# Summing the weights of the first MLP product on VectorE and GpSimd instead of in adding transfers

## The chip, the cores and the metric

The kernel runs on one core of one Trainium2 chip. The metric is the time of one execution in microseconds (us); less is better. Beside the engines the text speaks of queues: SP's queue issues plain loads, POOL's queue issues stores, the transfers that add into what they write, and whatever GpSimd computes. Both work strictly in the order in which their instructions stand. In the rows of the profile PE is TensorE, PEld its weight loads, DVE VectorE, ACT ScalarE, POOL GpSimd, and SPq or POOLq the issuing side of a queue.

## The reference

One layer of a hybrid backbone over 512 latent positions of width 2048, with 256 context tokens before them. What matters here is its last part:

```python
def squared_relu_mlp(h, w1, w2):
    return jnp.square(jax.nn.relu(h @ w1)) @ w2
...
xl = xl + gt2_l * squared_relu_mlp(modulate(rms_norm(xl, g_mlp[l]), sh2_l, sc2_l), w_mlp1[l], w_mlp2[l])
return rms_norm(xl, g_final)
```

`h` is 512x2048, `w1` 2048x8192 and `w2` 8192x2048, all in float32. Ahead of it stand the adaLN modulation (`silu(c) @ w_ada + b_ada`, six vectors of 2048), an input projection, a Fourier group, a state-space scan and an output projection. The last of the six modulation vectors, the gate `gt2_l`, is needed only in the second product.

## The kernel before

**Exact products by three passes.** A weight tile of 128x1024 is loaded raw and split into two parts, `whi` (ScalarE casts it, L84) and `wlo` (VectorE subtracts, L85). `mm3` (L106 to L108) then multiplies hi by hi, lo by hi and hi by lo. A weight tile can be used by TensorE only once its `wlo` is there, and the pool of split tiles holds three pairs: the split of a tile starts when TensorE has finished the tile three places before it.

**Seven products for eight.** Both MLP products cut the matrices into 2x2 blocks and use seven block products with sums of weight blocks in place of eight. `seven` (L858) delivers the seven weight tiles of one row of work in the order that its loop gives them. This text calls them by number, in that order: item 1 (block 11), 2 (block 12), 5 (the sum s of blocks 21 and 22), 6 (s plus block 11), 4 (block 22), 7 (block 21 plus block 11), 3 (s plus blocks 11 and 12). An item is 24 matmuls (8 pieces of 128, three passes), so a row is 168 matmuls. Items 6 and 3 are made by VectorE additions in place (`s_2`, L873, and `s_4`, L877). The two other sums, for items 5 and 7, are made by transfers: `load` with two blocks issues a plain load on SP's queue (L869) and then, on POOL's queue, one that adds a second block from HBM into the same tile (L867). A row thus moves seven blocks of 512 KB: five plain and two adding.

**The two stages.** The first product runs 32 rows. Three of them are done in a different way beforehand, from wide slabs of weights (`w_1s`, split at L99 and L100), while the activations are still being made; 29 rows go through `seven(w_1[...])`. Each ends with a store of its 512 KB of hidden values on POOL's queue (L931). The second product runs 8 chunks of 4, again through `seven`; its transfers and additions are not touched by the change.

**Other work in the rows.** The gate vector is computed in the background: `background(2)` at the end of a row runs two steps of `ada_rest` (L194 to L206). A step loads a tile of 512 KB on SP's queue and makes two VectorE passes over it into `adacc` (L200, one of each eight L198); after eight steps TensorE reduces the result with eight small matmuls (L204). There are 32 steps, so the first 16 of the 29 rows carry them and the last 13 do not. Below these are called gate rows and plain rows, and a gate row's tiles gate tiles. The first activations of the second product (`hr`, four loads, L951) are also loaded during rows 1 and 2.

**Buffers and order.** Raw weights and gate tiles share one pool of seven tiles of 512 KB. A scheduler assigns a free tile when it places an instruction and fixes the order on each engine; `tc.high_priority()` puts the weight work first. An instruction at the head of an engine's queue that waits holds up everything behind it on that engine.

Of the kernel before, what the change touches and what calls it, by code (L numbers as in the profile page):

```python
# [10 lines left out]
ALU = mybir.AluOpType  # L11
# [25 lines left out]
N1P = 3  # L37
# [17 lines left out]
def tile_hybrid_trunk(ctx, tc, xT, ctxT, cvec, ccol, vec, alog, w_ada, w_adr, w_ins, w_zs, w_in, w_dt, w_f, w_o,  # L55
                      w_1s, w_1, w_2, cst, sel_d, dft, cw_d, out):
    nc = tc.nc
    v = nc.vector
    s = nc.scalar
# [14 lines left out]
    def acc(n=L):  # L74
        return psa.tile([P, L], F32, name="acc")[:, :n]

    def bank():
        return psb.tile([P, 512], F32, name="bank")

    def split(raw):  # L80

        hi = pools["ws"].tile([P, HALF], F32R, name="whi")
        lo = pools["ws"].tile([P, HALF], F32R, name="wlo")
        s.copy(hi, raw)  # L84
        v.tensor_sub(lo, raw, hi.bitcast(F32))  # L85
        return hi, lo

    def raw_tile():
        return pools["wp"].tile([P, HALF], F32, name="wraw")
# [15 lines left out]
    def mm3(ps, a, b, first, last, on=False):  # L105
        te.matmul(ps, a[0], b[0], start=first, stop=False, skip_group_check=on)  # L106
        te.matmul(ps, a[1], b[0], start=False, stop=False, skip_group_check=on)  # L107
        te.matmul(ps, a[0], b[1], start=False, stop=last, skip_group_check=on)  # L108
# [168 lines left out]
    def background(n):  # L277
        for _ in range(min(n, len(todo))):
            todo.pop(0)()
# [265 lines left out]
    for g in range(NG):  # L545
        b_tok = cp.tile([P, NCC, P], F32, name="cb_tok")
        x_tok = cp.tile([P, NCC, HG * 64], F32, name="cx_tok")
        for i in range(4):
            t = T_B + g if i == 0 else T_X + g * 3 + i - 1
# [216 lines left out]
    def sumsq(accum, x, pool, k):  # L766
        if k == 0:
            s.activation(accum, x, AF.Square)
        else:
            q = pool.tile([P, L], F32, name="nq")  # L770
            s.activation(q, x, AF.Square)
            v.tensor_add(accum, accum, q)
# [82 lines left out]
    for ci in range(20, 24):  # L855
        todo.extend(ada_rest(ci, None, stg1))

    def seven(src, use):  # L858

        raw = {}  # L860

        def load(n, *ij):
            raw[n] = raw_tile()
            for a, (i, j) in enumerate(ij):
                d = src[i, j].rearrange("p a b -> p (a b)" if len(src.shape) == 5 else "p a b c -> p (a b c)")
                if a:
                    nc.gpsimd.dma_start(out=raw[n], in_=d, accum_op=ALU.add)  # L867
                else:
                    nc.sync.dma_start(out=raw[n], in_=d)  # L869
            return raw[n]  # L870

        def s_2():
            v.tensor_add(raw["s"], raw["s"], raw["11"])  # L873
            return raw["s"]

        def s_4():
            v.tensor_add(raw["s"], raw["s"], raw["12"])  # L877
            return raw["s"]

        for n, f in ((1, lambda: load("11", (0, 0))), (2, lambda: load("12", (0, 1))),  # L880
                     (5, lambda: load("s", (1, 0), (1, 1))), (6, s_2), (4, lambda: load("22", (1, 1))),
                     (7, lambda: load("t", (1, 0), (0, 0))), (3, s_4)):
            with tc.high_priority():
                w = split(f())
            use(n, w)
# [9 lines left out]
    for rr in range(N1P, NP):  # L895
        ct = stg.tile([P, 4, LC], F32, name="ct")
        sn = stg.tile([P, 4, LC], F32, name="sn")
        ps = {}

        def use(n, w):  # L900
            if n == 1:
                ps["x"] = acc(LC)
            elif n in (2, 5, 4):
                ps[{2: "y", 5: "z", 4: "w"}[n]] = bank()[:, :LC]
            o = ps[{1: "x", 6: "x", 7: "x", 2: "y", 5: "z", 3: "z", 4: "w"}[n]]
            for k in range(8):
                sl = slice(k * P, (k + 1) * P)
                i, q = k // QC, k % QC
                mm3(o, (w[0][:, sl], w[1][:, sl]), (chi[i][:, SLOT[n], q], clo[i][:, SLOT[n], q]),
                    k == 0 and n not in (6, 7, 3), k == 7, n not in (2, 4))  # L910
            if n == 1:
                s.copy(sn[:, 0], o)
            elif n == 2:
                v.tensor_add(ct[:, 0], sn[:, 0], o)
            elif n == 5:
                s.copy(sn[:, 3], o)
            elif n == 6:
                s.copy(sn[:, 1], o)
            elif n == 4:
                s.copy(sn[:, 2], o)  # L920
            elif n == 7:
                v.tensor_sub(ct[:, 2], o, sn[:, 2])
                v.tensor_add(ct[:, 3], o, sn[:, 3])
            else:
                v.tensor_add(ct[:, 1], sn[:, 1], o)

        seven(w_1[rr - N1P], use)
        s.activation(ct[:, 2:4], ct[:, 2:4], AF.Relu, scale=-1.0)
        s.activation(ct[:, 0:2], ct[:, 0:2], AF.Relu)
        s.activation(ct, ct, AF.Square)  # L930
        nc.gpsimd.dma_start(out=hid_d[rr // QC][:, :, rr % QC], in_=ct)  # L931
        background(2)
# [52 lines left out]
    for c in range(NFC):  # L985
        hi, lo = chi[c % 2], clo[c % 2]
        last = c == NFC - 1
        if last:
            hr_stack.close()
            comb0_stack.close()  # L990
            fin["p"] = ctx.enter_context(tc.tile_pool(name="fin", bufs=2))
            x2p = ctx.enter_context(tc.tile_pool(name="x2p", bufs=1))
            x2f = [x2p.tile([P, L], F32, name=f"x2f{j}") for j in range(KT)]
            fin["a"] = fin["p"].tile([P, L], F32, name="na2")
            fin["r"] = fin["p"].tile([P, L], F32, name="na2")
            for j in range(KT):
                jj = j // 2 + (j % 2) * 8
                nc.sync.dma_start(out=x2f[jj], in_=x2_d[jj])
        else:
            todo.extend(factors(c + 1))  # L1000
        for op in range(4):
            cts = [[stc.tile([P, 2, LC], F32, name=f"ca{i}{o}") for i in range(2)] for o in range(2)]
            sns = [stc1.tile([P, 3, LC], F32, name=f"sn{o}") for o in range(2)]
            pss = [{}, {}]

            def use2(n, w):
                wv = [w_.rearrange("p (q o m) -> p q o m", q=QC, o=2) for w_ in w]
                for o in range(2):
                    ps, ct, sn = pss[o], cts[o], sns[o]
                    j = 2 * op + o  # L1010
                    if n == 1:
                        ps["x"] = acc(LC)
                    elif n in (2, 5, 4):
                        ps[{2: "y", 5: "z", 4: "w"}[n]] = bank()[:, :LC]
                    d = ps[{1: "x", 6: "x", 7: "x", 2: "y", 5: "z", 3: "z", 4: "w"}[n]]
                    for q in range(QC):
                        mm3(d, (wv[0][:, q, o], wv[1][:, q, o]), (hi[:, SLOT[n], q], lo[:, SLOT[n], q]),
                            q == 0 and n not in (6, 7, 3), q == QC - 1, n not in (2, 4))
                    g0, g1, n1 = mod[:, 80 + j:81 + j], mod[:, 88 + j:89 + j], ng[:, j:j + 1]
                    if n == 1:  # L1020
                        s.activation(sn[:, 0], d, AF.Copy, scale=g0)
                    elif n == 2:
                        v.scalar_tensor_tensor(ct[0][:, 0], d, g0, sn[:, 0], ALU.mult, ALU.add)  # L1023
                    elif n == 5:
                        s.activation(sn[:, 2], d, AF.Copy, scale=g1)
                    elif n == 6:
                        s.activation(sn[:, 0], d, AF.Copy, scale=g0)
                    elif n == 4:
                        s.activation(sn[:, 1], d, AF.Copy, scale=g1)
                    elif n == 7:  # L1030
                        v.scalar_tensor_tensor(ct[1][:, 0], d, n1, sn[:, 1], ALU.mult, ALU.add)
                        v.scalar_tensor_tensor(ct[1][:, 1], d, n1, sn[:, 2], ALU.mult, ALU.subtract)
                    else:
                        v.scalar_tensor_tensor(ct[0][:, 1], d, g0, sn[:, 0], ALU.mult, ALU.add)

            seven(w_2[c, op], use2)
            for o in range(2):
                for i in range(2):
                    j = 2 * op + o + 8 * i
                    ct = cts[o][i].rearrange("p a b -> p (a b)")  # L1040
                    if last:
                        v.tensor_add(x2f[j], x2f[j], ct)
                        sumsq(fin["a"], x2f[j], fin["p"], op + o + i)
                    else:
                        nc.gpsimd.dma_start(out=x2_d[j], in_=ct, accum_op=ALU.add)
            background(2)
        background(len(todo))
# [86 lines left out]
```

## Time and profile before

| | us |
|---|---|
| median of 3 runs | 2385.83 (2382.52 to 2394.14) |
| the profiled execution | 2374.16 |
| its span (first to last instruction) | 2372.4 |
| TensorE busy in the span | 2262.6 (95%) |
| VectorE busy | 1811.1 (76%) |
| ScalarE busy | 1176.3 (50%) |
| GpSimd busy | 285.7 (12%) |
| adding weight loads in both MLP products | 122, of these 58 in the first |

The rows of the first product begin with TensorE at about 1072 us and end at about 1703 us; the second product follows to the end. One instruction marks the rows well: ScalarE's copy at L912, which stands once in every row, right after the row's first item. In a row of the trace's order of time the columns are start, duration, engine, line, operation, tiles and shapes, count, and in brackets the idle time ahead of it with what ended it. In a row of a grouped view they are busy time and mean nanoseconds, then the idle time before the group's instructions with what ended it.

### The profile page before, as it was taken

The numbers are of one execution on the slowest core, as the hardware profiler recorded it, in microseconds if no ns is written. First come the engines' busy times: TensorE is split into PE (matmuls) and PEld (weight loads), VectorE is DVE, ScalarE is ACT, GpSimd is POOL, SyncE is SP. The second block draws the span as 40 slices with busy tenths as digits, with TensorE's granted clock in tenths as the row PEclk, the third lists the DMA queues.
The fourth block names the chain that finished last, engine by engine and source line by source line (L and its number), as shares of the span: only waits on it lengthen the run. The fifth ranks groups of instructions, "written<-read, shape, count | busy, mean of one in ns | idle before, by whom it ended". The sixth has DMA issues, their size and how long they took to land.

```text
span 2372.4 us, 38829 instructions
## 1 busy us (share of the span) xinstructions
PE 2262.6 (95%) x15242; PEld 2004.8 (85%) x15242; DVE 1811.1 (76%) x2551; ACT 1176.3 (50%) x1646; POOL 285.7 (12%) x375
## 2 busy tenths in 40 slices
PE   6999999999999999898999999999999999999996
PEld 2347789877777777698999989999999999999995
DVE  7978779987778677675666666666898887888778
ACT  4125245456555422254444545555665665566554
POOL 0000000000000000111101101111122222222210
PEclk9999999999999999999999999999999999999998
DMA  8988877823224499557888877777899999999993
GB/s 297 333 296 299 330 240 261 279 83 122 83 63 148 144 345 303 187 163 230 253 224 244 239 217 220 208 209 213 242 264 267 266 250 267 259 265 247 242 267 116
DMA packets 163456, 544.72 MB, mean 230 GB/s; under 512 B 19284, under 2 KB 20196, under 8 KB 163016
## 3 DMA queue, kind: packets, MB, share of 16 engines
q1 hardware_dynamic: 115624, 402.35, 49.6%
q0 software_dynamic: 46496, 137.79, 27.1%
q8 instruction: 119, 1.95, 0.3%
q10 hardware_dynamic: 1152, 2.10, 0.2%
q14 instruction: 65, 0.53, 0.1%
HBM read 479.24 MB, written 62.92 MB: 229 GB/s over the span
## 4 chain that ended last, share of the span: by engine, by line
PE 63%; DVE 15%; DMA 14%; issue 4%; ACT 3%; SPq 0%; DVEq 0%; POOL 0%; ACTq 0%; POOLq 0%
PE acc L107 10%; PE acc L108 10%; PE acc L106 9%; PE bank L107 8%; PE bank L106 8%; PE bank L108 8%; DMA araw<-in_w_ada_dram 5%; DMA wraw<-in_w_adr_dram 3%; DVE araw L172 3%; DVE wlo L100 2%; DVE wlo L85 2%; DMA araw<-in_w_adr_dram 2%; DMA wraw<-in_w_o_dram 1%; PE bank L347 1%; PE bank L667 1%
## 5 line engine op out<-in xcount | busy, mean ns | idle before, releaser
L85 DVE TENSOR_TENSOR wlo<-wraw,whi 128x1024 fp32r<-128x1024 f32 x427 | 519.4, 1221 | 224.0 <-ACT whi L84 221.1
L84 ACT CAST whi<-wraw 128x1024 fp32r<-128x1024 f32 x427 | 445.4, 1048 | 448.8 <-PE bank L108 158.4
L107 PE MATMUL bank<-chi,wlo 128*128 128x256 f32 (+1 forms) x2000 | 569.7, 285 | 6.1 <-DVE wlo L85 6.1
L106 PE MATMUL bank<-chi,whi 128*128 128x256 f32 (+1 forms) x2000 | 569.6, 285 | 1.1 <-DVE ca L1023 0.8
L108 PE MATMUL bank<-clo,whi 128*128 128x256 f32 (+1 forms) x2000 | 569.3, 285 | 0.0
L107 PE MATMUL acc<-chi,wlo 128*128 128x256 f32 (+1 forms) x1512 | 435.7, 288 | 21.7 <-DVE wlo L85 21.5
L106 PE MATMUL acc<-chi,whi 128*128 128x256 f32 (+1 forms) x1512 | 433.4, 287 | 7.3 <-ACT chi L830 6.7
L108 PE MATMUL acc<-clo,whi 128*128 128x256 f32 (+1 forms) x1512 | 433.7, 287 | 0.0
L107 PEld LDWEIGHTS bank<-chi,wlo 128*128 128x128 f32 x2000 | 384.5, 192 | 7.7 <-DVE wlo L85 6.7
L106 PEld LDWEIGHTS bank<-chi,whi 128*128 128x128 f32 x2000 | 384.5, 192 | 2.6 <-DVE ca L1023 1.3
L108 PEld LDWEIGHTS bank<-clo,whi 128*128 128x128 f32 x2000 | 384.5, 192 | 0.9
L107 PEld LDWEIGHTS acc<-chi,wlo 128*128 128x128 f32 x1512 | 293.6, 194 | 25.7 <-DVE wlo L85 24.3
L106 PEld LDWEIGHTS acc<-chi,whi 128*128 128x128 f32 x1512 | 293.1, 194 | 9.5 <-ACT chi L830 7.6
L107 PE MATMUL acc<-bh,wlo 128*128 128x512 f32 x720 | 286.2, 397 | 13.3 <-DVE wlo L100 13.3
L108 PEld LDWEIGHTS acc<-clo,whi 128*128 128x128 f32 x1512 | 293.5, 194 | 1.6 <-DVE clo L832 0.6
L106 PE MATMUL acc<-bh,whi 128*128 128x512 f32 x720 | 285.3, 397 | 1.1 <-ACT whi L99 1.1
L108 PE MATMUL acc<-bl,whi 128*128 128x512 f32 x720 | 284.4, 395 | 0.0
L99 ACT CAST whi<-wraw 128x1024 fp32r<-128x1024 f32 (+2 forms) x145 | 142.7, 987 | 263.3 <-PE acc L108 228.6
L867 POOL DMA_DIRECT2D wraw<-in_w_dram x122 | 105.1, 861 | 757.1 <-DMA wraw<-in_w_dram 334.8
L100 DVE TENSOR_TENSOR wlo<-wraw,whi 128x1024 fp32r<-128x1024 f32 (+2 forms) x145 | 165.6, 1144 | 29.0 <-ACT whi L99 28.0
L107 PEld LDWEIGHTS acc<-bh,wlo 128*128 128x128 f32 x720 | 136.1, 189 | 48.2 <-DVE wlo L100 20.1
L106 PEld LDWEIGHTS acc<-bh,whi 128*128 128x128 f32 x720 | 136.0, 189 | 29.8 <-ACT whi L99 1.6
(336 smaller groups left out, 3274.0 us busy)
## 6 DMA issues: line engine op xcount, KB each, us to landing
wraw<-in_w_dram SPq DMA_DIRECT2D x305, 512.0 KB, 5.2
araw<-in_w_ada_dram SPq DMA_DIRECT2D x164, 512.0 KB, 6.7
wraw<-in_w_dram POOLq DMA_DIRECT2D x122, 512.0 KB, 8.0
wraw<-in_w_in_dram SPq DMA_DIRECT2D x84, 512.0 KB, 4.5
x<-ca POOLq DMA_DIRECT2D x112, 256.0 KB, 8.0
araw<-in_w_adr_dram SPq DMA_DIRECT2D x48, 512.0 KB, 4.6
wraw<-in_w_adr_dram SPq DMA_DIRECT2D x32, 512.0 KB, 7.7
hid<-ct POOLq DMA_DIRECT2D x32, 512.0 KB, 5.4
```

The source lines that it names most:

```text
L84: s.copy(hi, raw)
L85: v.tensor_sub(lo, raw, hi.bitcast(F32))
L99: s.copy(hi, raw)
L100: v.tensor_sub(lo, raw, hi.bitcast(F32))
L106: te.matmul(ps, a[0], b[0], start=first, stop=False, skip_group_check=on)
L107: te.matmul(ps, a[1], b[0], start=False, stop=False, skip_group_check=on)
L108: te.matmul(ps, a[0], b[1], start=False, stop=last, skip_group_check=on)
L172: v.tensor_tensor_reduce(o, a, cond[:, hf * HALF:(hf + 1) * HALF], 1.0, last if hf else first, ALU.mult, ALU.add, dst[:, ch:ch + 1] if hf ...
L347: te.matmul(a[:n], w[:, o:o + n], tmp, start=k == 0, stop=k == KT - 1)
L667: te.matmul(py[hh * 64:hh * 64 + 64, c * P:(c + 1) * P], xd[d][:, c, hh], ms[2 * hh + d][:, c], start=c == 0 and d == 0, stop=c == NCH - 1 ...
L867: nc.gpsimd.dma_start(out=raw[n], in_=d, accum_op=ALU.add)
```

## The change

In the first product, `seven` no longer loads sums. Blocks 21 and 22 are loaded plain, once each (tiles `t` and `22`); VectorE adds them into a new tile `s` for item 5 (`s_1`), item 4 uses the tile `22` that is already there, and for item 7 GpSimd adds block 11 into `t` in place (`s_3`). The second product keeps its adding transfers (`adds=True`).

```diff
-    def seven(src, use):
+    def seven(src, use, adds):
...
+        def s_1():
+            if adds:
+                return load("s", (1, 0), (1, 1))
+            load("t", (1, 0))
+            load("22", (1, 1))
+            raw["s"] = raw_tile()
+            v.tensor_add(raw["s"], raw["t"], raw["22"])
+            return raw["s"]
+
+        def w_22():
+            return load("22", (1, 1)) if adds else raw["22"]
+
+        def s_3():
+            if adds:
+                return load("t", (1, 0), (0, 0))
+            nc.gpsimd.tensor_tensor(raw["t"], raw["t"], raw["11"], ALU.add)
+            return raw["t"]
...
-        for n, f in ((1, lambda: load("11", (0, 0))), (2, lambda: load("12", (0, 1))),
-                     (5, lambda: load("s", (1, 0), (1, 1))), (6, s_2), (4, lambda: load("22", (1, 1))),
-                     (7, lambda: load("t", (1, 0), (0, 0))), (3, s_4)):
+        for n, f in ((1, lambda: load("11", (0, 0))), (2, lambda: load("12", (0, 1))), (5, s_1), (6, s_2), (4, w_22),
+                     (7, s_3), (3, s_4)):
             with tc.high_priority():
                 w = split(f())
             use(n, w)
...
-        seven(w_1[rr - N1P], use)
+        seven(w_1[rr - N1P], use, False)
...
-            seven(w_2[c, op], use2)
+            seven(w_2[c, op], use2, True)
```

A row now moves four blocks, all on SP's queue. Line numbers shift: L873 and L877 become L891 and L895, L914 becomes L931, L922 to L925 become L939 to L942, and L931 becomes L948. The order of TensorE's and ScalarE's work is unchanged. The order of three other engines follows, for the turn from one gate row to the next, the same row of the program before and after.

VectorE before, from the addition for item 3 (L877) to the split of the next row's item 2:

```order
L877 TENSOR_TENSOR wraw_9857<-wraw_9857,wraw_9825 128x1024
L85 TENSOR_TENSOR wlo_9923<-wraw_9920,whi_9922 128x1024
L85 TENSOR_TENSOR wlo_9956<-wraw_9952,whi_9955 128x1024
L85 TENSOR_TENSOR wlo_9987<-wraw_9857,whi_9986 128x1024
L200 SCALAR_TENSOR_TENSOR adacc_9782<-wraw_10255,cs_79,adacc_9782 128x512 x2
L85 TENSOR_TENSOR wlo_10032<-wraw_10029,whi_10031 128x1024
L200 SCALAR_TENSOR_TENSOR adacc_9782<-wraw_10259,cs_79,adacc_9782 128x512
L922 TENSOR_TENSOR ct_9791<-acc_9799,sn_9792 128x256
L923 TENSOR_TENSOR ct_9791<-acc_9799,sn_9792 128x256
L85 TENSOR_TENSOR wlo_10064<-wraw_10061,whi_10063 128x1024
```

VectorE in the changed program, the same stretch:

```order
L895 TENSOR_TENSOR wraw_9856<-wraw_9856,wraw_9820 128x1024
L85 TENSOR_TENSOR wlo_9919<-wraw_9854,whi_9918 128x1024
L85 TENSOR_TENSOR wlo_9950<-wraw_9852,whi_9949 128x1024
L878 TENSOR_TENSOR wraw_10091<-wraw_10087,wraw_10089 128x1024
L85 TENSOR_TENSOR wlo_9981<-wraw_9856,whi_9980 128x1024
L200 SCALAR_TENSOR_TENSOR adacc_9777<-wraw_10248,cs_79,adacc_9777 128x512 x2
L85 TENSOR_TENSOR wlo_10026<-wraw_10023,whi_10025 128x1024
L200 SCALAR_TENSOR_TENSOR adacc_9777<-wraw_10252,cs_79,adacc_9777 128x512
L939 TENSOR_TENSOR ct_9786<-acc_9794,sn_9787 128x256
L940 TENSOR_TENSOR ct_9786<-acc_9794,sn_9787 128x256
L85 TENSOR_TENSOR wlo_10058<-wraw_10055,whi_10057 128x1024
```

The splits of items 4, 7 and 3 stand as before; the new addition (L878) for the next row's item 5 stands between those of items 7 and 3, and waits there for the next row's blocks 21 (`wraw_10087`) and 22 (`wraw_10089`).

SP's queue before, the loads of one row and its two gate tiles:

```order
L869 DMA wraw_10029<-in_w_1_dram 128x1024
L869 DMA wraw_10061<-in_w_1_dram 128x1024
L869 DMA wraw_10093<-in_w_1_dram 128x1024
L869 DMA wraw_10156<-in_w_1_dram 128x1024
L869 DMA wraw_10188<-in_w_1_dram 128x1024
L194 DMA wraw_10255<-in_w_adr_dram 128x1024
L194 DMA wraw_10259<-in_w_adr_dram 128x1024
```

SP's queue in the changed program:

```order
L869 DMA wraw_10023<-in_w_1_dram 128x1024
L869 DMA wraw_10055<-in_w_1_dram 128x1024
L869 DMA wraw_10087<-in_w_1_dram 128x1024
L869 DMA wraw_10089<-in_w_1_dram 128x1024
L194 DMA wraw_10248<-in_w_adr_dram 128x1024
L194 DMA wraw_10252<-in_w_adr_dram 128x1024
```

The load for item 7 is gone from between the block 22 and the gate tiles. In both programs the first gate tile takes the buffer that the split of the preceding row's item 7 gives free, and the second the one that item 3's split gives free. In the changed program block 21 takes a buffer that the preceding row's addition for item 6 (L891) and GpSimd's addition leave, and block 22 one that the addition for item 3 (L895) leaves.

POOL's queue before, and then in the changed program, for the same rows:

```order
L867 DMA wraw_10093<-in_w_1_dram 128x1024
L867 DMA wraw_10188<-in_w_1_dram 128x1024
L931 DMA hid2_6732<-ct_9791 512x1x256
L867 DMA wraw_10329<-in_w_1_dram 128x1024
L867 DMA wraw_10424<-in_w_1_dram 128x1024
```

```order
L887 TENSOR_TENSOR wraw_10087<-wraw_10087,wraw_10023 128x1024
L948 DMA hid2_6732<-ct_9786 512x1x256
L887 TENSOR_TENSOR wraw_10322<-wraw_10322,wraw_10258 128x1024
L948 DMA hid2_6732<-ct_10021 512x1x256
L887 TENSOR_TENSOR wraw_10563<-wraw_10563,wraw_10499 128x1024
```

Two adding loads per row have become one addition, in front of the same store. It waits for L878 of its own row, which reads the tile that it overwrites.

## The prediction

> **What bounds the kernel now.** I first read the summary of engines. TensorE is busy for 95% of the span, so the change can only win where TensorE waits or runs slowly.
>
> ```profile
> PE 2262.6 (95%) x15242; PEld 2004.8 (85%) x15242; DVE 1811.1 (76%) x2551; ACT 1176.3 (50%) x1646; POOL 285.7 (12%) x375
> ```
>
> Next comes the order of time on ScalarE, where L912 marks each row of the first product: the first gate rows, then the first plain rows.
>
> ```profile
> 1075.00 0.37 ACT L912 COPY sn<-acc 128x256 f32<-128x256 f32 x1
> 1102.36 0.36 ACT L912 COPY sn<-acc 128x256 f32<-128x256 f32 x1
> 1129.25 0.37 ACT L912 COPY sn<-acc 128x256 f32<-128x256 f32 x1
> ...
> 1439.04 0.37 ACT L912 COPY sn<-acc 128x256 f32<-128x256 f32 x1 [1.05 <-PE acc L108]
> 1459.20 0.37 ACT L912 COPY sn<-acc 128x256 f32<-128x256 f32 x1 [0.16 <-PE acc L108]
> 1479.36 0.37 ACT L912 COPY sn<-acc 128x256 f32<-128x256 f32 x1 [0.16 <-PE acc L108]
> ```
>
> A plain row takes 20.16 us, which is 168 matmuls at 0.12 us: TensorE never waits there, and no saved transfer can make it shorter. The 16 gate rows take 1439.04 - 1075.00 = 364.04 us, where 16 x 20.16 = 322.56 would do. The excess is 41.5 us, 7.2 of it in row 0 (27.36 us) and 6.7 in row 1 (26.89 us). What it consists of, by TensorE's groups in these rows and by stretches around the wait in row 1 (columns: busy us of PE, PEld, DVE, ACT, POOL with counts, then granted clock, DMA share, GB/s):
>
> ```profile
> L107 PE MATMUL bank<-chi,wlo 128*128 128x256 f32 x512 | 146.0, 285 | 6.1 <-DVE wlo L85 6.1
> L107 PE MATMUL acc<-chi,wlo 128*128 128x256 f32 x376 | 110.4, 294 | 21.0 <-DVE wlo L85 21.0
> L204 PE MATMUL bank<-ones,adacc 128*128 128x2 f32 x32 | 3.8, 241 | 0.0
> ...
> 1118.00:1124.00 6.00, 0.00 (x0) 0.00 (x0) 2.62 (x4) 0.00 (x0) 0.85 (x1) 0.84 1.05 391
> 1124.00:1127.00 3.00, 2.94 (x13) 2.94 (x14) 3.00 (x6) 1.57 (x2) 0.00 (x0) 0.50 1.02 287
> 1130.00:1134.00 4.00, 4.00 (x36) 4.00 (x35) 3.03 (x4) 1.99 (x2) 0.28 (x1) 1.00 0.70 204
> ```
>
> TensorE waits 27.1 us for VectorE's `wlo`; the gate's own small matmuls are at most 3.8. Most of the rest is clock: after the wait in row 1 the granted clock is 0.50, and 13 matmuls pass in 3 us instead of 25. Why `wlo` is late shows on VectorE, in the turn between two gate rows:
>
> ```profile
> 1311.13 1.22 DVE L877 TENSOR_TENSOR wraw<-wraw 128x1024 f32<-128x1024 f32 x1
> 1312.27 1.22 DVE L85 TENSOR_TENSOR wlo<-wraw,whi 128x1024 fp32r<-128x1024 f32 x1
> 1313.96 1.23 DVE L85 TENSOR_TENSOR wlo<-wraw,whi 128x1024 fp32r<-128x1024 f32 x1 [0.48 <-ACT whi L84]
> 1316.89 1.22 DVE L85 TENSOR_TENSOR wlo<-wraw,whi 128x1024 fp32r<-128x1024 f32 x1 [1.70 <-ACT whi L84]
> 1322.92 1.54 DVE L200 SCALAR_TENSOR_TENSOR adacc<-wraw,cs,adacc 128x512 f32<-128x512 f32 x2 [4.81 <-DMA wraw<-in_w_adr_dram]
> 1324.37 1.22 DVE L85 TENSOR_TENSOR wlo<-wraw,whi 128x1024 fp32r<-128x1024 f32 x1
> ```
>
> VectorE stands 4.81 us in front of a gate tile, and the split behind it, the next row's item 1, is late. SP can issue that tile's load only when item 7's split (here 1313.96 to 1315.19) has given its buffer free, and it lands over 7 us later. The transfers of the gate rows (KB each, median us to landing), and one group from earlier in the kernel:
>
> ```profile
> wraw<-in_w_dram SPq DMA_DIRECT2D x74, 512.0 KB, 4.5
> wraw<-in_w_dram POOLq DMA_DIRECT2D x29, 512.0 KB, 8.0
> wraw<-in_w_adr_dram SPq DMA_DIRECT2D x28, 512.0 KB, 7.8
> ...
> araw<-in_w_adr_dram SPq DMA_DIRECT2D x28, 512.0 KB, 4.7
> ```
>
> The same gate tiles land in 4.7 us between 400 and 900 us, where less is under way. In the rows they start just behind the row's last plain load and beside the adding loads.
>
> **What the change removes.** A gate row's transfers go from 10 (seven blocks, two gate tiles, one store) to 7. Nothing plain or adding stands just ahead of the first gate tile any more. So I take 4.7 us for its landing instead of 7.8; the bounds are those two rows.
>
> **What it adds on VectorE.** One addition (L878) of the size of L877, between the splits of items 7 and 3. It waits there for the next row's blocks 21 and 22. Block 22 is the late one: its buffer comes free with the addition for item 3 (L895). Behind the waiting L878 stand item 3's split, the gate passes and the next row's splits. The durations in a gate row, back to back:
>
> ```profile
> 1335.16 2.35 DVE L85 TENSOR_TENSOR wlo<-wraw,whi 128x1024 fp32r<-128x1024 f32 x2
> 1325.51 0.74 DVE L200 SCALAR_TENSOR_TENSOR adacc<-wraw,cs,adacc 128x512 f32<-128x512 f32 x1
> 1326.17 0.41 DVE L922 TENSOR_TENSOR ct<-acc,sn 128x256 f32<-128x256 f32 x1
> 1309.66 1.23 DVE L85 TENSOR_TENSOR wlo<-wraw,whi 128x1024 fp32r<-128x1024 f32 x1 [1.11 <-ACT whi L84]
> ```
>
> Seven splits and three additions at 2.35 / 2 = 1.17 make 11.7; four gate passes at 0.74, 3.0; four small ones at 0.36 (half of 0.41 overlaps the next), 1.4. The cast of item 6 must follow the addition L891 and costs VectorE 1.1 of waiting. From the end of L895 block 22 needs 4.5, of which the splits of items 4 and 7 cover 2.3: a wait of 2.2. The sum is 19.4 us, under the 20.16 that TensorE needs. The first gate tile, issued at the end of item 7's split, lands after 4.7; until then VectorE has the rest of the wait, L878 and item 3's split (2.2 + 1.2 + 1.2 = 4.6), so that stall is covered. The second tile follows item 3's split and has the gate passes and two splits as cover.
>
> The bound is close: at a landing of 5.2 us the sum is 20.1, and each us above it is a us per gate row. The plain loads of the gate rows give the spread:
>
> ```profile
> DMA to landing us min/median/max: 3.3/4.5/8.1
> ```
>
> I take the median, because there is less traffic than in this row's stretch, and leave 0.3 us per row for late ones.
>
> In the plain rows the same addition has cover:
>
> ```profile
> 1482.67 1.22 DVE L877 TENSOR_TENSOR wraw<-wraw 128x1024 f32<-128x1024 f32 x1
> ...
> 1486.20 1.22 DVE L85 TENSOR_TENSOR wlo<-wraw,whi 128x1024 fp32r<-128x1024 f32 x1 [1.17 <-ACT whi L84]
> 1489.12 1.23 DVE L85 TENSOR_TENSOR wlo<-wraw,whi 128x1024 fp32r<-128x1024 f32 x1 [1.70 <-ACT whi L84]
> ```
>
> Item 1 of this row began about 1476.3 (2.88 before the copy at 1479.36, and 0.16 for the copy's start), so item 3's split is wanted by 1476.3 + 6 x 2.88 = 1493.6. Block 22, issued at 1483.9, lands at 1488.4; addition and split end at 1490.8. The cost is nothing, by VectorE's idle time, up to a landing of about 7 us. Beyond it each us costs 13 us over the plain rows.
>
> **What it adds on GpSimd.** One addition per row. The trace has no arithmetic on GpSimd, so its length is bounded: below by VectorE's 1.22 us for the same shape, above by the costliest row per column:
>
> ```profile
> L640 DVE SCALAR_TENSOR_TENSOR hs<-hs,dec,bank 128x64 f32<-128x64 f32 x96 | 21.0, 273 | 0.0
> L85 DVE TENSOR_TENSOR wlo<-wraw,whi x206: 1210/1224/1227, 1064.8 to 1700.1; 128x1024 fp32r<-128x1024 f32 x103
> ```
>
> 273 ns for 64 columns would be 4.4 us for 1024. The result is wanted some 17 us after it starts, so either end is hidden on POOL itself; POOL's stores behind it have a row's time. What it may do to VectorE lies between nothing and standing VectorE still for its whole length. I take nothing: over the whole stage the splits vary only from 1210 to 1227 ns, though POOL was building descriptors in those rows. That is no addition reading the same memory, so the other end stays as a rival. The first row's two additions fall into idle time, where one further instruction that POOL needs ahead of its first addition is hidden too:
>
> ```profile
> 1055.60 0.42 DVE L833 TENSOR_TENSOR l<-xa,h 128x256 fp32r<-128x256 f32 x1 [2.81 <-ACT h L831]
> 1072.67 0.78 POOL L894 DMA_DIRECT2D hid<-ct  x1 [14.54 <-ACT ct L893]
> ```
>
> **The sum.** At stake are 41.5 - 3.8 = 37.7 us. What stays: row 0, where VectorE waits for a store that the change leaves in place, about 4; row 1, where the four `hr` loads now stand around block 22 and the gate tiles, about 4; 14 rows at 0.3, 4.
>
> ```profile
> 1084.20 0.42 DVE L914 TENSOR_TENSOR ct<-sn,bank 128x256 f32<-128x256 f32 x1 [4.34 <-DMA hid<-ct]
> 1121.34 1.54 DVE L200 SCALAR_TENSOR_TENSOR adacc<-wraw,cs,adacc 128x512 f32<-128x512 f32 x2 [10.21 <-DMA wraw<-in_w_adr_dram]
> ```
>
> The gain is 37.7 - 12 = 26 us. Against the profiled execution's 2374.16 that is 2348. The median of the runs is 2385.83, 0.5% above the profiled one, and the prediction is for that: 2360. From nothing left in the rows (38) to twice what I leave (14) its own range is 2348 to 2372.
>
> **The rivals.** *GpSimd's addition stops VectorE.* Then its length is added to VectorE's sum in a gate row. At twice VectorE's duration, 2.4 us, the sum is 19.4 + 2.4 = 21.8, so 1.6 us over TensorE's 20.16. Fourteen rows lose 23 where they now lose 41.5 - 13.9 - 3.8 = 23.8, and only rows 0 and 1, where VectorE idles long enough for the addition, gain: 13.9 - 8, some 6 us: 2379. Plain rows hold 10 x 1.17 + 1.4 + 1.1 + 2.2 + 2.4 = 18.8 and stay with TensorE. For it speaks that L878, which releases the addition, stands right where VectorE is fullest; against it the even splits above. The Trainium skill says of this, in "SBUF — State Buffer", section "Who interferes with whom", that a VectorE instruction with two inputs in SBUF contends with a GpSimd instruction that reads SBUF, and that whichever starts second is blocked until the first ends. No run here shows it yet. "GPSIMD Engine Reference", section 3.1, has 4497 ns for such an addition over 2048 columns, so by that page an estimate of 2.25 us here and about 2377 us by this rival.
>
> *The same with a long addition* (slower): at 4.4 us a gate row takes 23.8 and a plain row 20.8. That is 14 x 3.6 + 13 x 0.6 = 58, with 12 for rows 0 and 1 and 3.8, against 41.5 now: 32 us more, 2418. It decides from an addition of about 2.6 us that stops VectorE wholly.
>
> *The gate tiles land as late as before.* If 7.8 us belong to these loads and not to their neighbours, VectorE's stop moves by the length of L878 and stays otherwise: 2386. The 4.7 us of the same tensor elsewhere speaks against it.
>
> **How the numbers follow.** My forecast gets 0.46, the stopped VectorE 0.28, the long addition 0.11, the late gate tiles 0.15. A measurement of this kernel can tell about 0.5% (12 us) from no change. Faster by more: 0.46 and 0.08 of the second, 0.54; within: 0.18 of the second and all of the fourth, 0.33; slower: the third and the remaining 0.02, 0.13. The range over the cases is 2345 to 2388: it begins a little below the forecast's own, for the scatter of the runs, and takes in the values of the second and fourth case; about 2 in 10 are left out, mostly above.
>
> **What would show it.** Gate rows of 20.2 to 20.6 us by the copies of the row marker; gate tiles landing in about 5 us; TensorE's wait for `wlo` down from 27 to under 10 us; clock 1.00 through these rows. VectorE's splits longer than 1.23 us would show the first rival, and GpSimd's addition its length. L878 waiting longer than 3 us for its block would show my landing wrong.

## The result, and the profile after

| | before | changed |
|---|---|---|
| median, first set of runs (us) | 2385.39 (2382.52 to 2394.14) | 2351.28 (2345.72 to 2356.04) |
| median, set of the last four experiments | 2386.57 (2379.86 to 2392.30) | 2347.75 (2339.27 to 2350.00) |
| ratio to before, first set | | 0.9848, 95% interval 0.9821 to 0.9875 |
| ratio to before, later set | | 0.9830, 95% interval 0.9810 to 0.9849 |
| the profiled execution (us) | 2374.16 | 2345.72 |
| the 16 gate rows in it (us) | 364.04 | 329.48 |

The change makes the kernel 1.5 to 1.7% faster, 34 to 39 us. The forecast was 2360 with a gain of 26: the sign was right and the gain too small.

In the order of time on ScalarE of the changed kernel, the row marker (now L929; start, duration, engine, line, operation, tiles) stands at the first gate rows and the first plain rows:

```profile
1078.63 0.37 ACT L929 COPY sn<-acc 128x256 f32<-128x256 f32 x1
1100.09 0.35 ACT L929 COPY sn<-acc 128x256 f32<-128x256 f32 x1
1122.45 0.35 ACT L929 COPY sn<-acc 128x256 f32<-128x256 f32 x1
...
1408.11 0.37 ACT L929 COPY sn<-acc 128x256 f32<-128x256 f32 x1 [0.76 <-PE acc L108]
1428.27 0.37 ACT L929 COPY sn<-acc 128x256 f32<-128x256 f32 x1 [0.15 <-PE acc L108]
1448.43 0.37 ACT L929 COPY sn<-acc 128x256 f32<-128x256 f32 x1 [0.15 <-PE acc L108]
```

From 1078.63 to 1408.11 are 329.48 us for 16 rows, 20.59 each; plain rows are at 20.16 as before. The excess over 16 x 20.16 fell from 41.5 to 6.9 us: 1.3 in row 0, 2.2 in row 1, and 3.4 in the other 14, no more than the gate's own small matmuls take there (at most 3.8). So 34.6 us went in these rows, which is the whole gain.

The next two fences give the 14 gate rows from the third marker on, first of before, then of the changed kernel: the stretch with busy us of PE, PEld, DVE, ACT and POOL, clock, DMA share and GB/s, and then VectorE's waits (total us, times, longest).

```profile
1129.25:1439.04 309.79, 292.51 (x2386) 290.56 (x2385) 204.97 (x240) 148.17 (x196) 35.31 (x43) 0.98 0.84 236
...
DVE adacc L200 <- DMA wraw<-in_w_adr_dram: 54.4, 13, 6.5
DVE wlo L85 <- ACT whi L84: 42.9, 46, 1.7
```

```profile
1122.45:1408.11 285.66, 284.38 (x2366) 283.56 (x2365) 242.91 (x255) 147.98 (x197) 56.46 (x29) 1.00 0.57 179
...
DVE wraw L878 <- DMA wraw<-in_w_dram: 21.3, 14, 2.3
DVE wlo L85 <- ACT whi L84: 15.3, 19, 1.1
DVE adacc L200 <- DMA wraw<-in_w_adr_dram: 4.9, 6, 1.6
```

VectorE's stop before the gate tiles fell from 54.4 to 4.9 us, and TensorE is now busy for 284.38 of 285.66 us at full clock. But VectorE has become full as well: 242.91 busy and 21.3 + 15.3 + 4.9 waiting make 284.4 us. Its busy time grew by 37.9 us, and only 14 x 1.17 = 16.4 of that is the added L878. The rest shows in VectorE's groups from 1075 to 1440 us (busy us, mean ns, idle before), of before and then of the changed kernel, and below them GpSimd's addition over the whole stage (min/median/max ns). The stretch holds the 16 gate rows of before; in the changed kernel, whose gate rows end at 1408, it also takes in one and a half plain rows.

```profile
L85 DVE TENSOR_TENSOR wlo<-wraw,whi 128x1024 fp32r<-128x1024 f32 x112 | 135.8, 1220 | 46.3 <-ACT whi L84 46.3
L200 DVE SCALAR_TENSOR_TENSOR adacc<-wraw,cs,adacc 128x512 f32<-128x512 f32 x59 | 44.1, 748 | 70.8 <-DMA wraw<-in_w_adr_dram 70.2
```

```profile
L85 DVE TENSOR_TENSOR wlo<-wraw,whi 128x1024 fp32r<-128x1024 f32 x124 | 164.3, 1337 | 24.5 <-ACT whi L84 24.4
L200 DVE SCALAR_TENSOR_TENSOR adacc<-wraw,cs,adacc 128x512 f32<-128x512 f32 x60 | 61.1, 1018 | 6.8 <-DMA wraw<-in_w_adr_dram 6.3
```

```profile
L887 POOL TENSOR_TENSOR wraw<-wraw x29: 2397/3257/3314, 1057.8 to 1639.6; 128x1024 f32<-128x1024 f32 x29
```

The splits' mean went from 1220 to 1337 ns (1313 in the 16 gate rows alone) and the gate passes' from 748 to 1018. One row shows how, on VectorE and then on GpSimd:

```profile
1316.61 1.22 DVE L85 TENSOR_TENSOR wlo<-wraw,whi 128x1024 fp32r<-128x1024 f32 x1
1318.14 3.04 DVE L85 TENSOR_TENSOR wlo<-wraw,whi 128x1024 fp32r<-128x1024 f32 x1 [0.31 <-ACT whi L84]
1321.10 0.41 DVE L939 TENSOR_TENSOR ct<-acc,sn 128x256 f32<-128x256 f32 x1
```

```profile
1316.84 3.25 POOL L887 TENSOR_TENSOR wraw<-wraw 128x1024 f32<-128x1024 f32 x1 [8.41 <-DVE wraw L878]
```

GpSimd's addition is released at 1316.84 while a split runs; it ends 3.25 us later, where one that starts beside no split takes 2.40. So it stands about 0.85 us, roughly until the split ends at 1317.83. The next split, begun at 1318.14, ends at 1321.18, about 1 us after the addition, and takes 3.04 in place of 1.22. The mechanism of the first rival is there, and the kernel is faster all the same. How the two fit together is the question for the experiments.

Last, the changed kernel's transfers in the same stretch, 1075 to 1440 us (KB each, median us to landing): the loads of blocks, the gate tiles, the stores and the four loads of `hr`.

```profile
wraw<-in_w_dram SPq DMA_DIRECT2D x73, 512.0 KB, 4.0
wraw<-in_w_adr_dram SPq DMA_DIRECT2D x30, 512.0 KB, 3.6
hid<-ct POOLq DMA_DIRECT2D x20, 512.0 KB, 5.2
hr<-hid SPq DMA_DIRECT2D x4, 512.0 KB, 5.5
```

A gate tile lands in 3.6 us where it took 7.8.

### The profile page after: what moved, and what is told of

The parts are those of the page before. It is cut to its first block, busy times and chain, and to the rows that moved or that the text cites. A ratio compares the mean times of both kernels' runs of the same rounds, so it can differ in the third digit from the quotient of the medians.

```text
span 2343.9 us, 38720 instructions
## 1 busy us (share of the span) xinstructions
PE 2254.9 (96%) x15242; PEld 1996.9 (85%) x15242; DVE 1893.3 (81%) x2580; ACT 1175.0 (50%) x1646; POOL 319.9 (14%) x346
## 5 line engine op out<-in xcount | busy, mean ns | idle before, releaser
L85 DVE TENSOR_TENSOR wlo<-wraw,whi 128x1024 fp32r<-128x1024 f32 x427 | 552.1, 1302 | 164.7 <-ACT whi L84 161.9
L108 PEld LDWEIGHTS acc<-bl,whi 128*128 128x128 f32 x720 | 135.4, 188 | 27.6 <-issue 0.8
```

## The experiments

Three theories stood against each other. **T1**: the adding transfers made the gate tiles late, and their removal is the gain. **T2**: GpSimd's blocking of VectorE is what is left, and is worth removing. **T3**: the gain comes from the new order and buffers, not from less traffic. The row times below are from the profiled execution of each kernel, between the row markers; "gate rows" is the sum of all 16. The landing of the gate tiles is the median from 1075 to 1440 us. Medians and intervals are over all runs.

| | gate rows (us) | gate tile lands (us) | median (us) | ratio to before, 95% interval |
|---|---|---|---|---|
| before | 364.0 | 7.8 | 2385 to 2387 | |
| changed | 329.5, again 329.7 | 3.6 | 2351.28, again 2347.75 | 0.9821 to 0.9875, again 0.9810 to 0.9849 |
| before without its adding transfers | 331.5 | 3.9 | 2347.94 | 0.9824 to 0.9872 |
| changed without GpSimd's addition | 327.2 | 3.6 | 2345.36 | 0.9812 to 0.9856 |
| changed, that addition on VectorE | 327.6, again 327.6 | 3.6 | 2343.29, again 2346.15 | 0.9801 to 0.9847, again 0.9816 to 0.9846 |
| changed, item 7's adding transfer kept | 345.0 | 5.2 | 2355.29 | 0.9848 to 0.9904 |
| changed, item 5's adding transfer kept | 350.8 | 7.3 | 2371.31 | 0.9914 to 0.9946 |
| changed, GpSimd adds twice | 357.3 | 3.5 | 2375.50 | 0.9952 to 0.9988 |

### Before, only without the adding transfers

```diff
-                if a:
+                if a and len(src.shape) == 5:
+                    continue
+                elif a:
```

> The kernel before with only the first product's two adding transfers per row left out; the tiles for items 5 and 7 then hold one block in place of a sum, so part of the computation is missing. Order of all other instructions as before, no new arithmetic. Theory T1 (the gain comes from the traffic that is gone: the gate tiles then land in about 4 us in place of 7.8 and VectorE no longer stands before them): gate rows 20.2 to 20.8 us, total about 2345 to 2352. Theory T3 (the gain comes from the new order and the buffers that it leaves): gate tiles still land in over 6 us, total stays at 2380 to 2388.

Gate rows came to 331.5 us (20.72 each), the total to 2347.94. VectorE's groups and the transfers of the gate tiles and of `hr` in this kernel, again from 1075 to 1440 us:

```profile
L85 DVE TENSOR_TENSOR wlo<-wraw,whi 128x1024 fp32r<-128x1024 f32 x124 | 151.3, 1222 | 75.4 <-ACT whi L84 75.1
L200 DVE SCALAR_TENSOR_TENSOR adacc<-wraw,cs,adacc 128x512 f32<-128x512 f32 x60 | 44.9, 749 | 24.3 <-DMA wraw<-in_w_adr_dram 23.3 <-DVE wlo L85 0.3
```

```profile
wraw<-in_w_adr_dram SPq DMA_DIRECT2D x30, 512.0 KB, 3.9
...
hr<-hid SPq DMA_DIRECT2D x4, 512.0 KB, 9.2
```

Nothing but the adding transfers was taken away, with POOL's issuing of them and the waits for them; order and plain loads stayed, item 7's load just ahead of the gate tiles among them. The tiles land in 3.9 us, VectorE's stop before them falls from 70.8 to 24.3, and nearly the whole gain is there (32.6 of 34.6 us in the gate rows). From row 2 on all of it is there: these 14 rows take 285.2 us, and 285.7 in the changed kernel. Rows 0 and 1 take 46.3 us here, 43.8 in the changed kernel and 54.2 before: the four `hr` loads still land late, in 9.2 us, and VectorE still waits 11.3 us for gate tiles in these two rows. So T1 holds, and T3 falls but for some 2.5 us in rows 0 and 1.

### One adding transfer kept

Item 7's:

```diff
-            nc.gpsimd.tensor_tensor(raw["t"], raw["t"], raw["11"], ALU.add)
+            nc.gpsimd.dma_start(out=raw["t"], in_=src[0, 0].rearrange("p a b -> p (a b)"), accum_op=ALU.add)
```

> The changed kernel with one of the two adding transfers back: block 11 is added into block 21 by a transfer on POOL's queue in place of GpSimd's arithmetic; item 5's sum stays on VectorE. Orders on VectorE and SP as in the changed kernel. T1 (traffic): the gate tiles, which start beside this transfer, land in 4.5 to 6 us, VectorE stands before them for 1 to 2 us, gate rows 20.6 to 21.6, total 2350 to 2366. T2 (the blocking is worth more than the traffic): splits at 1.22 us, gate rows 20.2 to 20.4, total below the changed kernel by 2 to 5 us. T3 (order and buffers): as the changed kernel, within 2 us.

Item 5's:

```diff
-            if adds:
-                return load("s", (1, 0), (1, 1))
-            load("t", (1, 0))
-            load("22", (1, 1))
-            raw["s"] = raw_tile()
-            v.tensor_add(raw["s"], raw["t"], raw["22"])
-            return raw["s"]
+            return load("s", (1, 0), (1, 1))
...
-            return load("22", (1, 1)) if adds else raw["22"]
+            return load("22", (1, 1))
...
+            load("t", (1, 0))
             nc.gpsimd.tensor_tensor(raw["t"], raw["t"], raw["11"], ALU.add)
```

> The other half of the change alone: item 5's sum is again made by an adding transfer, with blocks 21 and 22 each loaded a second time for items 7 and 4; item 7's sum is made by GpSimd. VectorE's order is that of the kernel before (no L878), with GpSimd's addition on top. In the two runs so far a gate row of the changed kernel took 20.6 us and one with item 7's adding transfer kept took 21.6. If each adding transfer costs alike wherever it runs: gate tiles land in 5 to 6 us, gate rows 21.2 to 21.8 us (339 to 349 us for 16). If only the one that runs beside the gate tiles counts (item 7's): gate tiles land in under 4.5 us, gate rows 20.3 to 20.8.

Gate rows took 345.0 us (21.56 each) with item 7's and 350.8 (21.93) with item 5's: 15.6 and 21.4 us more than the changed kernel. Together that is 36.9, about what both cost in the kernel before (34.6). The totals make the first one smaller: 4 to 8 us above the changed kernel with item 7's, whose profiled execution (2362.23) was the slowest of its four, and 20 to 24 with item 5's. So what item 7's costs alone is known only to lie between some 4 and 16 us. The kernel with item 5's also loads block 21 a second time and has no L878; the kernel of the first experiment, with as many plain loads and no L878 either, took only 2.0 us more than the changed kernel in these rows, so most of the 21.4 is the adding transfer's. Its gate tiles (7.3 us) and rows lie above what I expected if both cost alike. That only item 7's counts is refuted: item 5's does at least as much. This is a turn between two rows in the kernel with item 5's transfer kept: SP's gate tiles, POOL's adding transfer of the next row's item 5 (start of its issue), and VectorE.

```profile
1310.86 3.20 SPq L194 DMA_DIRECT2D wraw<-in_w_adr_dram  x2
...
1310.31 0.87 POOL L867 DMA_DIRECT2D wraw<-in_w_dram  x1 [5.89 <-DMA wraw<-in_w_dram]
...
1317.52 1.54 DVE L200 SCALAR_TENSOR_TENSOR adacc<-wraw,cs,adacc 128x512 f32<-128x512 f32 x2 [3.82 <-DMA wraw<-in_w_adr_dram]
```

And the kernel with item 7's kept, where the issue of the two gate tiles spans 1303.61 to 1307.68:

```profile
1303.61 4.07 SPq L194 DMA_DIRECT2D wraw<-in_w_adr_dram  x2
...
1306.49 0.87 POOL L887 DMA_DIRECT2D wraw<-in_w_dram  x1 [8.59 <-DVE wraw L878]
...
1307.69 1.54 DVE L200 SCALAR_TENSOR_TENSOR adacc<-wraw,cs,adacc 128x512 f32<-128x512 f32 x2 [0.37 <-DMA wraw<-in_w_adr_dram]
1309.15 1.22 DVE L85 TENSOR_TENSOR wlo<-wraw,whi 128x1024 fp32r<-128x1024 f32 x1
1314.63 0.75 DVE L200 SCALAR_TENSOR_TENSOR adacc<-wraw,cs,adacc 128x512 f32<-128x512 f32 x1 [4.26 <-DMA wraw<-in_w_adr_dram]
```

POOL issues item 5's addition for the next row within a microsecond of the first gate tile, which VectorE then gets 6.7 us after its issue. Item 7's starts when the first tile is nearly in (VectorE waits 0.37 for it) and falls on the second (4.26). Each adding transfer makes the gate tile beside it late; the kernel before had both.

Their price can be read in the plain rows, where no gate tile runs. The rows are of DMA queues in 1439 to 1640 us (packets, MB, share of sixteen engines' time; q0 holds stores and adding transfers, q1 plain loads), of before, of the changed kernel, and with item 7's transfer kept:

```profile
q0 software_dynamic: 4369, 15.87, 38.5%
q1 hardware_dynamic: 7200, 26.22, 36.5%
```

```profile
q0 software_dynamic: 1440, 5.24, 9.3%
```

```profile
q0 software_dynamic: 2880, 10.49, 23.9%
```

Before has 20 adding transfers more than the changed kernel there: 29.2% of 201 us over 20 is 2.93 us of all sixteen engines for each. The kernel with item 7's has 10 more: 14.6% of 201 us over 10 is again 2.93. A plain block costs 36.5% of 201 us over 50, 1.47. So an adding transfer holds the engines twice as long as a plain one of the same size.

### GpSimd's addition left out, moved, and doubled

Left out (one line less) and moved to VectorE:

```diff
-            nc.gpsimd.tensor_tensor(raw["t"], raw["t"], raw["11"], ALU.add)
+            v.tensor_add(raw["t"], raw["t"], raw["11"])
```

> The changed kernel without GpSimd's addition: item 7 uses block 21 alone, so one addition of the computation is missing. Order on VectorE and SP as in the changed kernel. T2 (GpSimd's addition blocks VectorE, and that is most of what is left in the gate rows): VectorE's splits back to 1.21 to 1.23 us, gate rows from 20.6 to 20.2 to 20.3 us, 3 to 5 us less than the changed kernel, about 2347. T1 alone (the blocked time is hidden under TensorE's 20.16 us): splits also back to 1.22, but the time within 1.5 us of the changed kernel. If the splits stay long, GpSimd is not what stretches them.

> The changed kernel with the addition for item 7 on VectorE in place of GpSimd. T2: VectorE pays 1.17 us a row for it in place of about 1.7 us of being blocked, so VectorE's sum falls by some 0.5 us: gate rows 20.3 to 20.5, total 2 to 4 us less than the changed kernel, about 2348. If the blocked time is hidden: within 1.5 us. If GpSimd's addition had been free for VectorE: 1.2 us more per gate row, about 2365.

Without the addition the splits of the gate rows are even again, and gate rows take 327.2 us. The splits' durations in the gate rows without it, and in the changed kernel (min/median/max ns):

```profile
L85 DVE TENSOR_TENSOR wlo<-wraw,whi x113: 1209/1224/1227, 1073.8 to 1400.0; 128x1024 fp32r<-128x1024 f32 x113
```

```profile
L85 DVE TENSOR_TENSOR wlo<-wraw,whi x113: 1207/1218/3436, 1077.0 to 1405.8; 128x1024 fp32r<-128x1024 f32 x113
```

GpSimd's addition is what stretches them, by up to 3436 - 1224 = 2212 ns. In 14 gate rows VectorE's busy time is 223.66 us without it:

```profile
1118.00:1402.63 284.63, 284.58 (x2374) 284.38 (x2373) 223.66 (x255) 149.63 (x197) 10.68 (x15) 1.00 0.56 180
```

Against the 242.91 above, the blocking costs VectorE (242.91 - 223.66) / 14 = 1.4 us a row, and the time only 2.3 us over all 16 rows. TensorE is busy for 284.58 of 284.63 us here, so VectorE's room comes to nothing. T2 is right about the mechanism and wrong about its worth. On VectorE itself the addition costs 1.2 us a row in place of 1.4, and the gate rows are 1.9 and 2.0 us shorter than the changed kernel's in two pairs of profiles. The same first product ran once more in the kernel with both products changed (below), with gate rows of 331.9 us, so differences of this size are known only to some 2 us. The totals don't part the two:

> The changed kernel itself, once more, beside the three others of this set on one chip: it shows how far the time and the gate rows (20.59 us on average in the first profile) come back. Gate rows again 329 to 331 us for 16; total 2343 to 2355.

> Item 7's addition on VectorE once more, against the changed kernel in the same set. The rows of the first product were shorter by 1.9 us in its first profile, its median by 8. If the rows tell all of it: 1 to 3 us below the changed kernel, which the intervals will not part. If there is more in it that the rows do not show: 6 to 10 us below.

In this set the changed kernel had 2347.75 and the one with VectorE 2346.15, with nearly the same intervals. The 8 us between the medians of two earlier sets did not come back.

Doubled (the same line twice):

> The changed kernel with GpSimd's addition done twice in each row (block 11 is added two times, so the sums for item 7 are not the ones wanted). Orders on VectorE and SP as in the changed kernel. If the blocking is real and VectorE is at its limit in the gate rows: 1.7 to 2.4 us more per gate row, rows of 21.8 to 22.8 us, total 18 to 36 us above the changed kernel; plain rows stay at 20.16. If VectorE has room left: gate rows grow by under 0.5 us, total within 8 us of the changed kernel.

Gate rows took 357.3 us (22.33 each) and the total was 2375.50, 24 to 28 above the changed kernel; the gate tiles still landed in 3.5. VectorE in one row and over 14:

```profile
1295.86 5.69 DVE L200 SCALAR_TENSOR_TENSOR adacc<-wraw,cs,adacc 128x512 f32<-128x512 f32 x2
...
1129.23:1438.29 309.06, 291.11 (x2367) 288.50 (x2366) 269.90 (x255) 147.96 (x198) 96.13 (x42) 0.98 0.51 166
```

Two gate passes that take 1.54 took 5.69. VectorE's busy time grew by another 27.0 us over the 14 rows, and the rows by 309.06 - 285.66 = 23.4. So VectorE was at its limit with one addition, and most of what a second one takes from it is paid in time. In the gate rows it takes back 27.8 of the 34.6 us. The Trainium skill says, in "SBUF — State Buffer", section "Who interferes with whom", that a VectorE instruction with two inputs in SBUF contends with a GpSimd instruction that reads SBUF and that the second waits for the first. These traces agree, both ways round: GpSimd waits 0.85 us behind a split, and a split or gate pass waits up to 2.2 us behind the addition of 2.40.

### The gate steps spread over all rows

One edit, made to the changed kernel and to the kernel before:

```diff
-        background(2)
+        background(2 if rr < N1P + 3 else 1)
```

> The changed kernel with the gate steps spread over all 29 rows (two in each of the first three, then one per row) in place of two in each of the first 16. Same work, other places. If what is left in the gate rows is VectorE's sum being at TensorE's 20.16 us: a row with one gate tile has 1.5 us less VectorE work and half the gate loads, rows of 20.16 to 20.3 from row 3 on, 2 to 4 us less than the changed kernel. If what is left is elsewhere (rows 0 and 1, the gate's own matmuls): within 1.5 us.

> The kernel before with the gate steps spread in the same way, adding transfers kept. T1 (gate tiles landing late beside the adding transfers, and VectorE standing before them): with one gate tile per row VectorE has a pass and a split less in the row, so most of the 14 rows' 27 us of excess goes even though the tile still lands late; total 2352 to 2368. If each gate tile that lands late costs its stall alone, wherever it stands, the 32 stalls are only moved: within 5 us of the kernel before.

On the changed kernel the 28 steps of the row marker took 571.1 us where they had taken 572.0; the median was 2345.93 (ratio to before 0.9823 to 0.9879). This is within what was to be told apart. On the kernel before they took 604.7 in place of 606.5, and the time was 2392.94, ratio 1.0038 (1.0016 to 1.0061): 0.4%, 8 us, slower. Here I missed: neither of my two cases had a loss. The profiled execution (2377.54) was the fastest of ten and shows where the stops stand, but not where the loss comes from, which stays open. Who waited for the gate tiles from 1130 to 1680 us of that kernel (us, times), and their landing:

```profile
  DVE adacc L200: 97.5, 23
...
DMA to landing us min/median/max: 5.2/7.2/8.3
```

Over the 26 rows of this stretch VectorE stands 97.5 / 26 = 3.8 us a row before one tile, where it stood 54.4 / 14 = 3.9 a row before two. The second tile of a row had cost little (6.8 of the 54.4 us); the stop belongs to the turn between two rows, and spreading made 29 such turns out of 16. The row that I had costed as cheaper by a pass still has nearly the whole stop: it takes 21.2 us, where a row with two tiles took 22.1.

Both edits together, the addition on VectorE and the spreading:

> Item 7's addition on VectorE and the gate steps spread over all 29 rows. TensorE's own work in the 28 steps of the row marker is about 569 us (28 x 20.16, the last one's 0.55 and the gate's 3.8); the changed kernel took 572, the two edits alone 570 and 571. Expected 569 to 570, so 2 to 3 us below the changed kernel at most, and within 2 us of the edit on VectorE alone: what the rows could still give is used up. Any more would have to come from rows 0 and 1.

The 28 steps took 570.0 us and the median was 2345.99. From row 4 on every row takes 20.16 us, 0.9 more where the gate's small matmuls stand in it, so TensorE is the bound. By its total none of these versions is told apart from the changed kernel.

### The second product too

```diff
-            seven(w_2[c, op], use2, True)
+            seven(w_2[c, op], use2, False)
```

> The change carried on to the second product: there too VectorE and GpSimd make the sums for items 5 and 7, no adding transfers are left. VectorE has little room there: if its sum per row of work plus 1.2 us for the addition and 1.7 us of being blocked goes over TensorE's time, the second product's 32 rows lose up to 2 us each, total 20 to 60 us above the changed kernel. If late loads are what limits the second product: up to 15 us less than the changed kernel.

The median was 2387.07, ratio to before 1.0020 (0.9999 to 1.0041), 36 to 39 us above the changed kernel. The stage from the last row marker to the end went from 693.4 to 733.7 us. VectorE's groups there, in the changed kernel and in this one:

```profile
L85 DVE TENSOR_TENSOR wlo<-wraw,whi 128x1024 fp32r<-128x1024 f32 x222 | 269.9, 1222 | 96.0 <-ACT whi L84 93.4
```

```profile
L85 DVE TENSOR_TENSOR wlo<-wraw,whi 128x1024 fp32r<-128x1024 f32 x224 | 308.4, 1386 | 22.8 <-ACT whi L84 21.8
L878 DVE TENSOR_TENSOR wraw<-wraw 128x1024 f32<-128x1024 f32 x31 | 37.9, 1223 | 32.2 <-DMA wraw<-in_w_dram 32.1
L982 DVE TENSOR_TENSOR hr<-hr,hr 128x1024 f32<-128x1024 f32 x7 | 21.8, 3111 | 0.0
```

The added L878 takes 37.9 and waits 32.2, the splits grow by 38.5, and L982, 8.5 in the changed kernel, by 13.3: together 121.9 us. VectorE's old slack before the splits, 96.0, shrinks to 22.8 and takes up 73.2 of them; the stage grew by 40.3. What the addition, its wait and the blocking would each cost alone was not run. So in this kernel the adding transfers are the better choice in the second product, where VectorE has no room for the sums, and the arithmetic in the first, where the adding transfers make the gate tiles late.

## Why the prediction came out as it did

**What is at stake.** 37.7 us of excess beside the gate's own matmuls: right. The floor that I worked out, 322.56 + 3.8 = 326.4 us, is nearly what the kernel without GpSimd's addition reached (327.2).

**The gate tiles.** The mechanism was right: the tiles are late because of what runs beside them. The size was off. I took 4.7 us from tiles of the same tensor elsewhere, and they landed in 3.6, below the row that I took as the bound. I had counted transfers, ten down to seven; but each of the two adding ones weighed as two. What slowed the tiles of that other row is not shown. One plain load does still stand just ahead of the first gate tile, other than I wrote: that of block 22. In the turn shown above SP issued the tile at 1314.14, and L878 started at 1315.47, with the block in.

**VectorE's sum.** 11.7 + 3.0 + 1.4 = 16.1 us of work in a row: 223.66 / 14 = 15.98 without GpSimd's addition. The wait for the cast, 1.1: 15.3 / 14 = 1.1. The wait for block 22, 2.2: 21.3 / 14 = 1.5, since blocks landed in 4.0 where I took 4.5. The gate tiles, nothing: 0.35. That is 18.9 where I had 19.4.

**GpSimd's addition.** Its length lies between my bounds, 2.40 us. "I take nothing" for its effect on VectorE is the step that failed: it is 1.4 us a row. My reason, that splits were even while POOL built descriptors, was about another kind of work, as I said myself. With it the sum is 20.3 us, at TensorE's 20.16 and not under it, so the failed step cost only some 2 us. That it cost so little was luck in part: the blocks landed sooner than I had taken, which left VectorE the 0.5 us a row that it needed. The first rival had the mechanism but not the price: 19.4 + 2.4 = 21.8 counts the whole addition, while by this difference 1.0 us of it fell where VectorE was waiting anyway, and the rest of the sum was 0.5 shorter. Doubling the addition gave rows of 22.1 us, so the point from which that rival decides was close.

**What stays.** I left 12 us: 4 in row 0, 4 in row 1, 4 in the other 14. They measured 1.3, 2.2, and nothing: the 3.4 us of the other 14 are the gate's own matmuls, whose four groups stand in these rows and add 0.9 us each. This is the term that was mis-sized most, and it is all of the miss in the gate rows. In row 0 VectorE no longer waits for the store, which I had taken as left in place: L931 (L914 before) is not among VectorE's waits in rows 0 and 1, and the three stores just ahead land in 4.0 us (median; longest 6.5) where they took 4.7 (7.7). The change doesn't touch these stores; they got faster when the adding transfers went, for without these alone they land in 4.0 (6.2) and the wait is gone as well. In row 1 the four `hr` loads land in 5.5 where they took 10.5. That is not the adding transfers alone: without these, and with all five plain loads, they land in 9.2, and with four plain loads and item 7's adding transfer in 7.0. A plain load fewer, and the order and buffers that go with it, count at least as much there; the runs don't part these. VectorE's waits in rows 0 and 1 of the changed kernel:

```profile
DVE wraw L878 <- DMA wraw<-in_w_dram: 5.0, 2, 3.4
DVE wlo L85 <- ACT whi L84: 2.6, 2, 1.5
DVE adacc L200 <- DMA wraw<-in_w_adr_dram: 1.5, 1, 1.5
```

**The plain rows.** As predicted, 20.16 us as before, although GpSimd blocks VectorE there as well.

**The total.** The gain in the gate rows was 34.6 where I had 26, and 2360 - 8.6 is 2351.4, the median measured. The profiled execution came out nearer to its forecast (2345.72 for 2348) only by chance: it began the rows 3.6 us later and took 2.5 us longer in the second product than that of before, in stretches that the change doesn't touch. In its repeat the rows began at 1075.35, 0.35 from before.

## What to carry to other kernels

Cost a transfer by the time that it holds the queues' engines, not by its bytes or its count, and look which other transfers run beside it: here two adding loads made late a tile and a store that had nothing to do with them. Before arithmetic is moved to GpSimd, add its whole length to VectorE's sum in the fullest row, as an upper bound, and ask how much of it falls into VectorE's waits; where VectorE has no slack most of it is paid (here 23.4 us in 14 rows for a second addition, 1.7 of its 2.40 a row). When a stop belongs to a place in the row and not to the amount of work, spreading the work multiplies the stop.

## What the runs showed of the hardware that I had not expected

- An adding transfer of 512 KB from HBM into SBUF held the sixteen DMA engines for 2.93 us, a plain one for 1.47. Why it takes twice as long was not tried.
- GpSimd's addition of 128x1024 floats took 2.40 us when it started beside no split and 3.26 (median) when it was released while a split ran; a split behind it took up to 3.44 us in place of 1.22, a gate pass up to 2.88 in place of 0.75. These took turns with it by whole instructions.
- With the change carried to the second product, another VectorE addition of two tiles (L982), 1.22 us in the changed kernel, had a mean of 3.11. VectorE instructions with one input in SBUF and one in PSUM, TensorE's result memory, were spared: where GpSimd adds twice, L941 runs inside one of its additions in 11 rows, and in all 29 rows it takes 0.41 to 0.42 us.
